# A streaming encoder layer on one core: the last norm with tokens on partitions and two store queues, the last 64 SWA keys on four quarters of the array

## The chip, the cores and the metric

The kernel runs on one core of a Trainium2 chip. TensorE (PE) does the matrix products, VectorE (DVE), ScalarE (ACT) and GpSimd (POOL) work element by element, SyncE (SP) issues most of the transfers, and 16 DMA engines move the data. The metric is the device time of one execution in microseconds (us), lower is better.

## The reference

One inference step of one encoder layer, for a prompt of 1024 frames and a sample of 64 frames, together 1088 tokens of width 1024, everything in float32:

```python
xn = rms_norm(x, g_attn); rq, rk, rv, rg, sq, sk, sv, ga, gb = split(xn @ w_in)
a = (rms_norm(retention(rq, rk, rv)) * silu(rg)) @ w_ret_out       # 4 heads of 256
b = swa_attend(sq, sk, sv) @ w_swa_out                             # sliding-window attention (SWA)
x += (sigmoid(ga) * a + sigmoid(gb) * b) @ w_mix_out
x += cross_attn(rms_norm(x, g_cross), memory)                      # 4 heads, 256 memory tokens
x += (silu(hn @ w_gate) * (hn @ w_up)) @ w_down                    # hn = rms_norm(x, g_ffn)
y = rms_norm(x, g_final)
```

Two places of it matter here. In the SWA a chunk of 64 queries sees 192 keys (its own chunk and the two before), with 16 query heads of 64 in 2 groups, each group with one key and one value head; the outcome for a group is p @ v with p of 512 rows (8 heads x 64 queries) by 192 keys and v of 192 keys by 64. There are 17 chunks, 16 of the prompt and one of the sample; the first two of the prompt see fewer keys. The last norm is y * rsqrt(mean(y * y) + 1e-6) * g_final over the 1024 features of a token.

## The kernel before

Activations lie with features on partitions: eight tiles of 128 features by 1088 tokens. Most products are split into a high part (rounded to the matmul type fp32r) and a low part, and made as three products (`mm3`, L156 to L158): high by high, high by low, low by high. A weight unit of 128 output features is loaded as `raw`, cast on ACT to the high part (L123) and subtracted on DVE for the low part (L124); SWA's own products are plain f32 ones.

The stages follow one another: projections (to some 811 us), SWA with filler (to some 1020), the merge of both branches, cross attention, and a feed-forward part with Strassen products, which ends in the norm (`finish`).

**SWA** (`swa`) runs over half chunks, 34 of them, in a hand-written pipeline; `in_order` and `issue_after` chain each piece behind the last matmul issued, so that PE's order is the one written out. For each half chunk there are `scores` (L969, and the softmax: L979/L982 on DVE, exponentials L990 on ACT, the division L996 on POOL), two steps later `turn` (transposes of the probabilities on PE, L1008 for the first 128 keys and L1018 for the last 64; copies L1012 on ACT and L1020 on DVE into `pT`), and, for every second half, `weigh` (L1031): p @ v for all 16 heads. `weigh` has two stages. Stage 1 has the first 128 keys, all 128 rows of the array and, for each value head v, 64 of its columns: two products of 512 columns. Stage 2 has the last 64 keys: value head 0 with the rows and columns 0 to 63, value head 1 with the rows and columns 64 to 127, again two products of 512 columns. They add into one PSUM bank, `pout`, which L1035 copies out on DVE:

```python
po = pw.tile([P, 512], F32, tag="out", name="pout")
for j, part in enumerate(parts):
    for v, (val, pT) in enumerate(part):
        self.last_mm = mm(po[rows[v], :], val[:, rows[v]], pT, start=j == 0, stop=j == len(parts) - 1).ins
```

In each step stand pieces of **filler** work (`filler`), which fills PE while the softmax goes on: the product with `w_ret_out`, in groups of one weight unit m by one chunk of tokens c (384, 384 and 320 columns). A group takes one PSUM bank `pd` from a pool of three (`plain_psum`), is run in two halves, and is evacuated on DVE (L1187), where it is multiplied by a gate and then stored to `d_mix`. Units 0 and 1 come with the first groups, units from m = 2 on are loaded when their first group's turn comes in the program; the buffers of `raw` are two, so that a unit's load waits for the casts of the unit two before. PSUM has eight banks; the SWA's own pool has five (`pss` 2, two for the transposes, `pout`) and `pd` three. The pool `pd` stays through the merge and the cross attention.

**The tail** (`finish`). The 1088 tokens are three ranges of columns: c = 0 and c = 1 (272 each) and c = 2 (544, whose product is done before). `grow` adds the last product to y (L1639) and squares it on ACT (L1643), `gather` sums the squares (L1648), and the norm is then made in one of two ways. For c = 2 and c = 0, `sums` (L1656) gives the sum over features by matmuls with the squares as weights and ones as data, so that tokens lie on partitions (128 x 3 or 128 x 5 numbers); `roots` makes 1/sqrt of these in five steps with one Newton step (`steps`, L1721 to L1726, the square root on ACT, L1722); `spread` (L1682, L1685) spreads the factors back along the partitions. For c = 1, the last to come, `wide_roots` (L1670, L1671) multiplies a matrix of ones by the squares, so that every partition has all sums, and makes the same five steps on 128 x 272 numbers. Each `scale` (L1689, DVE) multiplies a tile by its gain and the factors, and stores it through SP's queue (L120). `queued` chains DVE's work in the order written.

## Time and profile before

| | us |
|---|---|
| median of 3 runs (lowest, highest) | 2211.39 (2210.66, 2214.1) |
| profiled execution, its own time | 2210.58 |
| its span in the profile | 2208.8 |
| mean granted TensorE clock | 0.992 |

Line numbers L... are those of the kernel before. In the rows of a timeline stand the start and the length in us, the engine, the line, the operation, the tiles (written <- read), the shape and the number of records; in brackets what the engine was idle for and what released it. In the rows of groups stand the busy time, the mean of one in ns, and the idle time before them. PEld is TensorE's weight load, SPq SyncE's queue of transfers. Names like `pout` are those of the program's tiles.

### The profile page before, as it was taken

What the parts mean: (1) busy time and instruction counts of PE and PEld (TensorE: products, weight loads), DVE (VectorE), ACT (ScalarE), POOL (GpSimd) and SP (SyncE); (2) the same over time, 40 slices, a digit from 0 to 9 for tenths busy, and PEclk for the clock granted to TensorE, in tenths of its full rate; (3) what the DMA queues carried; (4) which work ended last, traced back from release to release, by engine and by line L of the source; (5) the groups of instructions that cost most, each with busy time, mean ns of one, the idle gap of its engine ahead of it and who ended that gap; (6) DMA issues with size and microseconds to landing.
All of it is one profiled execution on the core that took longest, in us unless ns stands there. A gap on an engine that the chain in (4) does not pass through costs nothing.

```text
span 2208.8 us, 41446 instructions
## 1 busy us (share of the span) xinstructions
PE 2155.7 (98%) x16307; PEld 2089.8 (95%) x16307; DVE 1577.8 (71%) x2654; ACT 875.8 (40%) x1894; POOL 653.2 (30%) x442
## 2 busy tenths in 40 slices
PE   8999999999999998999999999999999999999996
PEld 8999999999999996779999999999999999999996
DVE  7996958776677668775455555768777776778498
ACT  7344424344344346553133333333322222344243
POOL 1322333332343122230000000014555555544440
PEclk9999999999999999999999999999999999999998
DMA  5534253445245476327443111422333332385233
GB/s 197 167 127 137 90 149 122 131 127 156 96 153 172 165 220 213 112 64 224 124 153 107 57 49 58 144 86 90 124 133 101 104 118 95 124 297 167 91 114 110
DMA packets 181444, 290.83 MB, mean 132 GB/s; under 512 B 40290, under 2 KB 109314, under 8 KB 181250
## 3 DMA queue, kind: packets, MB, share of 16 engines
q1 hardware_dynamic: 176706, 278.74, 39.5%
q10 hardware_dynamic: 4032, 7.80, 0.9%
q8 instruction: 129, 2.11, 0.4%
q0 software_dynamic: 512, 1.64, 0.2%
q14 instruction: 65, 0.53, 0.1%
HBM read 196.95 MB, written 91.16 MB: 130 GB/s over the span
## 4 chain that ended last, share of the span: by engine, by line
PE 80%; DVE 11%; DMA 4%; ACT 2%; issue 2%; POOL 1%; SPq 0%; DVEq 0%; ACTq 0%; POOLq 0%
PE pq L215 15%; PE pq L212 15%; PE pq L213 15%; PE pd L156 8%; PE pd L158 8%; PE pd L157 8%; DVE wq L124 1%; PE pout L1031 1%; PE pss L969 1%; DMA hl<-d_op 1%; DVE T L124 1%; DVE B L124 1%; PE pp L1008 1%; DMA qs<-d_qkv 1%; DVE stage L596 1%
## 5 line engine op out<-in xcount | busy, mean ns | idle before, releaser
L124 DVE TENSOR_TENSOR wq<-raw,wq 128x512 fp32r<-128x512 f32 (+1 forms) x499 | 441.2, 888 | 137.1 <-ACT wq L123 135.5
L123 ACT CAST wq<-raw 128x512 fp32r<-128x512 f32 (+1 forms) x499 | 303.6, 614 | 586.0 <-PE pq L215 244.8
L212 PE MATMUL pq<-T,wq 128*128 128x272 f32 x1832 | 490.8, 288 | 3.6 <-ACT wq L123 2.1
L213 PE MATMUL pq<-T,wq 128*128 128x272 f32 x1832 | 491.5, 288 | 0.0
L213 PE MATMUL pq<-B,wq 128*128 128x272 f32 x1592 | 429.6, 290 | 6.7 <-DVE B L124 6.7
L212 PE MATMUL pq<-B,wq 128*128 128x272 f32 x1592 | 427.4, 289 | 1.3 <-DVE stage L596 1.1
L215 PE MATMUL pq<-T,wq 128*128 128x272 f32 x1832 | 382.0, 289 | 0.9 <-DVE wq L124 0.9
L190 POOL TENSOR_TENSOR raw<-raw 128x512 f32<-128x512 f32 (+1 forms) x59 | 90.2, 1529 | 967.1 <-DVE rs_r L301 480.4
L212 PEld LDWEIGHTS pq<-T,wq 128*128 128x128 f32 x1832 | 344.1, 188 | 5.6 <-ACT wq L123 1.9
L213 PEld LDWEIGHTS pq<-T,wq 128*128 128x128 f32 x1832 | 344.1, 188 | 0.8 <-issue 0.7
L215 PE MATMUL pq<-B,wq 128*128 128x272 f32 x1592 | 332.8, 289 | 0.0
L213 PEld LDWEIGHTS pq<-B,wq 128*128 128x128 f32 x1592 | 300.7, 189 | 9.2 <-DVE B L124 8.3
L212 PEld LDWEIGHTS pq<-B,wq 128*128 128x128 f32 x1592 | 300.5, 189 | 1.8 <-ACT wq L123 1.3
L215 PEld LDWEIGHTS pq<-T,wq 128*128 128x128 f32 x1832 | 289.6, 189 | 1.6 <-DVE wq L124 1.1
L215 PEld LDWEIGHTS pq<-B,wq 128*128 128x128 f32 x1592 | 252.8, 190 | 0.8 <-issue 0.8
L259 DVE TENSOR_TENSOR u<-pq,u 128x544 f32<-128x544 f32 x177 | 127.5, 720 | 101.3 <-PE pq L215 100.4
L193 POOL TENSOR_TENSOR raw<-raw 128x512 f32<-128x512 f32 (+1 forms) x59 | 82.8, 1403 | 110.4 <-DVE wq L124 105.3
L596 DVE TENSOR_TENSOR stage<-pq,u 128x544 f32<-128x544 f32 x112 | 80.4, 718 | 34.6 <-PE pq L215 31.2
L191 POOL TENSOR_TENSOR raw<-raw 128x512 f32<-128x512 f32 (+1 forms) x59 | 90.4, 1533 | 3.5
L996 POOL TENSOR_TENSOR t<-t,den 128x768 f32<-128x768 f32 (+2 forms) x34 | 49.9, 1468 | 127.0 <-DVE den L994 51.9
L196 POOL TENSOR_TENSOR raw<-raw 128x512 f32<-128x512 f32 (+1 forms) x59 | 82.4, 1397 | 4.4
L990 ACT ACTIVATE t<-t,nm 128x192 f32<-128x192 f32 (+2 forms) x136 | 58.9, 434 | 45.5 <-DVE nm L985 45.5
(388 smaller groups left out, 4600.4 us busy)
## 6 DMA issues: line engine op xcount, KB each, us to landing
hl<-d_op SPq DMA_DIRECT2D x85, 272.0 KB, 4.7
d_qkv<-stage SPq DMA_DIRECT2D x44, 272.0 KB, 2.2
d_op<-stage SPq DMA_DIRECT2D x44, 272.0 KB, 2.1
d_op<-ht SPq DMA_DIRECT2D x44, 272.0 KB, 3.3
raw<-w_gate SPq DMA_DIRECT2D x22, 512.0 KB, 3.5
raw<-w_up SPq DMA_DIRECT2D x22, 512.0 KB, 3.7
raw<-w_down SPq DMA_DIRECT2D x16, 512.0 KB, 4.1
d_gate<-stage ACTq DMA_DIRECT2D x28, 272.0 KB, 2.9
```

What stands on the lines that cost most here:

```text
L123: self.last_cast = self.nc.scalar.copy(hi, src).ins
L124: return self.nc.vector.tensor_tensor(out=lo, in0=src, in1=hi.bitcast(F32), op=ALU.subtract).ins
L156: mm(ps, wh, xh, start=start, stop=False)
L157: mm(ps, wh, xl, start=False, stop=False)
L158: self.last_mm = mm(ps, wl, xh, start=False, stop=stop).ins
L190: tt(out=a11, in0=a11, in1=a21, op=sub)
L191: tt(out=a21, in0=a21, in1=a22, op=add)
L212: mm(ps[:, c, :HC], w[:, 0, ks], x[:, 0, cs], start=start, stop=False)
L213: mm(ps[:, c, :HC], w[:, 0, ks], x[:, 1, cs], start=False, stop=False)
L215: self.last_mm = mm(ps[:, c, :HC], w[:, 1, ks], x[:, 0, c * HC:(c + 1) * HC], start=False, stop=stop).ins
L259: add = lambda out, a, b: nc.vector.tensor_tensor(out=out, in0=a, in1=b, op=ALU.add)
L596: nc.vector.tensor_tensor(out=o, in0=ps, in1=sb, op=ALU.add)
```

## The change

There are three parts.

*SWA.* `pout` becomes two banks, of which 256 columns each are used; each 512-column product is split into two of 256 columns (h = 0, 1: the first and the second half of `pT`), bank h taking half h. Stage 1 then has four products. In stage 2 the transposes of the second half of a chunk (hf = 1) put the two value heads on the opposite rows, so that the four products of stage 2 stand on four different quarters of the array: for h = 0 (rows 0 to 63, head 0) and (rows 64 to 127, head 1), for h = 1 (rows 64 to 127, head 0) and (rows 0 to 63, head 1). For the bank, the pool `pd` has two in place of three during SWA; the merge and the cross attention have three as before.

*Filler.* The third weight unit (m = 2) is made under `issue_after(first)`, where `first` is the evacuation L1187 of the first group. On DVE its low parts then stand behind that evacuation. The load of the unit two later, which needs the same buffer, comes later on SP, behind a load of queries and one store of `d_mix`.

*Tail.* `wide_roots` is gone; c = 1 goes by `sums`, `roots` and `spread` as the others do. `sums` takes the last tile's squares as a second product in the same accumulation. The scales of c = 0, and those of c = 1 on DVE, read the factors from PSUM where `spread` put them (c = 0 has no copy on ACT). One scale of c = 0 stands between the square root and the reciprocal of c = 1. The last tile of c = 2 gets its gain on ACT (`gain`) and its factors on POOL (`aside`), and so do three of the eight tiles of c = 1 (third, fifth and eighth in order). The eight stores of c = 1 go alternately through SP's and ACT's queues.

```diff
@@ -395,8 +395,10 @@
                 self.sixth, self.turns, self.held, self.last_held = None, 0, [], 0
                 self.wp = self.left.enter_context(tc.tile_pool(name="weights", bufs=2, reuse_waits="tile"))
                 self.project_phase()
+                with self.plain_psum(2, side="right"):
+                    self.swa_phase()
                 with self.plain_psum(side="right"):
-                    self.mix_phase()
+                    self.merge_swa()
                     self.mem.close()
                     self.cross_phase()
                 rp = sctx.enter_context(tc.tile_pool(name="rf", bufs=1, reuse_waits="tile", side="right"))
@@ -410,9 +412,9 @@
         self.fp = ctx.enter_context(self.tc.tile_pool(name="fa", bufs=1, reuse_waits="tile"))
 
     @contextmanager
-    def plain_psum(self, **where):
+    def plain_psum(self, bufs=3, **where):
         with ExitStack() as ctx:
-            pd = ctx.enter_context(self.tc.tile_pool(name="pd", bufs=3, reuse_waits="tile", space=PSUM, **where))
+            pd = ctx.enter_context(self.tc.tile_pool(name="pd", bufs=bufs, reuse_waits="tile", space=PSUM, **where))
             self.dense_psum = lambda: pd.tile([P, 512], F32, tag="d", name="pd")
             yield
 
...
@@ -1010,29 +1011,32 @@
                     live[c, "T"] = [self.pw2.tile([P, 2, 512], F32, tag="pT0", name="pT"), self.pw2.tile([P, 512], F32, tag="pT1", name="pT")]
                 pT = live[c, "T"][0][:n]
                 nc.scalar.copy(pT[:, :, hf * 256:(hf + 1) * 256], pp[:n, :].rearrange("p (v i) -> p v i", v=2))
-                parts = [[(vt[0][:n], pT[:, v, :]) for v in range(2)]]
+                cs = [slice(h * 256, (h + 1) * 256) for h in range(2)]
+                parts = [[(h, v, vt[0][:n], pT[:, v, cs[h]]) for h in range(2) for v in range(2)]]
                 if nk == NKEY:
                     pp = pw.tile([P, 512], F32, tag="pt1", name="pp")
-                    for v, i in reversed(units):
-                        k0, n = (64, P) if v else (P, 64)
-                        self.last_mm = nc.tensor.transpose(pp[:n, i * P:(i + 1) * P], t[:, v, i, k0:k0 + n], self.ident).ins
+                    for r in (1, 0):
+                        k0, n = (64, P) if r else (P, 64)
+                        for i in range(2):
+                            self.last_mm = nc.tensor.transpose(pp[:n, i * P:(i + 1) * P], t[:, r ^ hf, i, k0:k0 + n], self.ident).ins
                     pT = live[c, "T"][1]
                     nc.vector.tensor_copy(pT[:, hf * 256:(hf + 1) * 256], pp[:, :256])
-                    parts.append([(vt[2 - v][rows[v]], pT[rows[v]]) for v in range(2)])
+                    parts.append([(h, r ^ h, vt[2 - r][rows[r]], pT[rows[r], cs[h]]) for h in range(2) for r in (h, 1 - h)])
                 live[c, "parts"] = parts
 
             def weigh(c, hf):
                 if hf == 0:
                     return
                 parts = live.pop((c, "parts"))
-                po = pw.tile([P, 512], F32, tag="out", name="pout")
+                po = pw.tile([P, 2, 512], F32, tag="out", name="pout")
                 for j, part in enumerate(parts):
-                    for v, (val, pT) in enumerate(part):
-                        self.last_mm = mm(po[rows[v], :], val[:, rows[v]], pT, start=j == 0, stop=j == len(parts) - 1).ins
+                    for h, v, val, pT in part:
+                        self.last_mm = mm(po[rows[v], h, :256], val[:, rows[v]], pT, start=j == 0, stop=j == len(parts) - 1).ins
                 if c % 2 == 0:
                     outs["osb"] = sw.tile([P, KT, 2, 64], F32, tag="osb", bufs=2, name="osb")
                 osb = outs["osb"]
-                nc.vector.tensor_copy(osb[:, :, c % 2, :], po.rearrange("p (m q) -> p m q", q=64))
+                nc.vector.tensor_copy(osb[:, :, c % 2, :].rearrange("p (h m) q -> p h m q", h=2),
+                                      po[:, :, :256].rearrange("p h (m q) -> p h m q", q=64))
                 if c % 2 == 1 or c == 16:
                     n = 128 if c % 2 == 1 else 64
                     c0 = (c // 2) * P
@@ -1174,7 +1178,11 @@
             for m, c in order:
                 c0, n = CH[c]
                 if m not in units:
-                    units[m] = self.unit(io["w_ret_out"][m], KT)
+                    if m == 2:
+                        with tc.issue_after(first):
+                            units[m] = self.unit(io["w_ret_out"][m], KT)
+                    else:
+                        units[m] = self.unit(io["w_ret_out"][m], KT)
                 u, g = units[m], ld()
                 self.load(g[:, :n], self.d_gate[1][m, :, c0:c0 + n])
                 for ps in self.pieces(u, rets, c0, n):
@@ -1184,7 +1192,9 @@
                     step += 1
                     if ps is None:
                         yield
-                nc.vector.tensor_tensor(out=g[:, :n], in0=ps, in1=g[:, :n], op=ALU.mult)
+                ins = nc.vector.tensor_tensor(out=g[:, :n], in0=ps, in1=g[:, :n], op=ALU.mult).ins
+                if step == 2:
+                    first = ins
                 self.store(self.d_mix[m, :, c0:c0 + n], g[:, :n])
                 yield
 
@@ -1647,32 +1657,25 @@
             acc = self.rstd[:, cols[c]]
             self.queued(lambda: tt(out=acc, in0=acc, in1=squares[c, m], op=ALU.add))
 
-        def sums(c):
+        def sums(c, *more):
 
             spans = self.spans(cols[c].stop - cols[c].start)
             ps = bank()[:, :2 * len(spans)].rearrange("p (t two) -> p t two", two=2)
+            parts = [self.rstd[:, cols[c]], *more]
             for i, (a, w) in enumerate(spans):
-                a += cols[c].start
-                self.last_mm = nc.tensor.matmul(ps[:, i, :], self.rstd[:, a:a + w], self.ones[:, :2], start=True, stop=True).ins
+                for j, x in enumerate(parts):
+                    self.last_mm = nc.tensor.matmul(ps[:, i, :], x[:, a:a + w], self.ones[:, :2], start=j == 0,
+                                                    stop=j == len(parts) - 1).ins
             r = self.np.tile([P, 5], F32, tag="rf", bufs=2, name="rs_f")[:, :len(spans)]
             factors[c] = r, spans, ps[:, :, 0]
 
-        def roots(c):
+        def roots(c, between=None):
             r, spans, ps = factors[c]
             v = self.np.tile([P, 5], F32, tag="vf", bufs=2, name="rf_v")[:, :len(spans)]
             t = self.np.tile([P, 5], F32, tag="tf", bufs=2, name="rf_t")[:, :len(spans)]
-            self.steps(r, v, t, ps)
-
-        def wide_roots(c, m):
-
-            ps = bank()[:, :HC]
-            mm = nc.tensor.matmul
-            mm(ps, self.ones, self.rstd[:, cols[c]], start=True, stop=False)
-            self.last_mm = mm(ps, self.ones, squares[c, m], start=False, stop=True).ins
-            v, t = (self.hl.tile([P, HALF], F32, tag="hl", name="wide")[:, :HC] for _ in range(2))
-            self.steps(self.rstd[:, cols[c]], v, t, ps)
-
-        def spread(c):
+            self.steps(r, v, t, ps, between)
+
+        def spread(c, copied=True):
             r, spans, _ = factors[c]
             for part in ((0, 2), (2, 5)) if len(spans) > 4 else ((0, len(spans)),):
                 pb = bank()
@@ -1682,12 +1685,24 @@
                     self.last_mm = nc.tensor.matmul(pb[:, at:at + P], r[:, i:i + 1].broadcast_to([P, P]), self.ident,
                                                     start=True, stop=True).ins
                 c0 = cols[c].start
-                nc.scalar.copy(self.rstd[:, c0 + a0:c0 + a1], pb[:, :a1 - a0])
-
-        def scale(c, k):
+                if copied:
+                    nc.scalar.copy(self.rstd[:, c0 + a0:c0 + a1], pb[:, :a1 - a0])
+            return pb
+
+        def scale(c, k, by=None, queue=nc.sync):
             o = y[k][:, cols[c]]
-            self.queued(lambda: stt(o, o, self.gains[:, 3, k:k + 1], self.rstd[:, cols[c]], ALU.mult, ALU.mult))
-            self.store(self.io["o_y"][k, :, cols[c]], o)
+            by = self.rstd[:, cols[c]] if by is None else by
+            self.queued(lambda: stt(o, o, self.gains[:, 3, k:k + 1], by, ALU.mult, ALU.mult))
+            queue.dma_start(self.io["o_y"][k, :, cols[c]], o)
+
+        def gain(c, k):
+            o = y[k][:, cols[c]]
+            nc.scalar.mul(o, o, self.gains[:, 3, k:k + 1])
+
+        def aside(c, k, queue=nc.sync):
+            o = y[k][:, cols[c]]
+            nc.gpsimd.tensor_tensor(out=o, in0=o, in1=self.rstd[:, cols[c]], op=ALU.mult)
+            queue.dma_start(self.io["o_y"][k, :, cols[c]], o)
 
         for j in range(2 * KT):
             c, m = divmod(j, KT)
@@ -1704,22 +1719,40 @@
                 self.in_order(lambda: sums(0))
                 roots(0)
             if j == KT + 6:
-                self.in_order(lambda: spread(0))
-            if j >= KT:
-                scale(2, j - KT)
-        for k in range(3):
-            scale(0, k)
-        self.in_order(lambda: wide_roots(1, rest[-1][0]))
+                pb0 = self.in_order(lambda: spread(0, False))[:, :HC]
+            if c and m < KT - 1:
+                scale(2, m)
+            if c and KT - 5 < m < KT - 1:
+                gain(1, rest[m][0])
+            if j == 2 * KT - 2:
+                gain(2, KT - 1)
+                aside(2, KT - 1)
+        m = rest[-1][0]
+        spare = [rest[i][0] for i in range(KT - 4, KT - 1)]
+        scale(0, 0, pb0)
+        scale(0, 1, pb0)
+        self.in_order(lambda: sums(1, squares[1, m]))
+        roots(1, lambda: scale(0, 2, pb0))
         for k in range(3, KT):
-            scale(0, k)
-        for k in range(KT):
-            scale(1, k)
-
-    def steps(self, out, v, t, ps):
+            scale(0, k, pb0)
+        pb = self.in_order(lambda: spread(1))[:, :HC]
+        queues = [nc.sync, nc.scalar]
+        rows = [k for k in range(KT) if k not in spare]
+        for i, k in zip((2, 4, 7), spare):
+            rows.insert(i, k)
+        for i, k in enumerate(rows):
+            if k in spare:
+                aside(1, k, queues[i % 2])
+            else:
+                scale(1, k, pb, queues[i % 2])
+
+    def steps(self, out, v, t, ps, between=None):
         nc = self.nc
         stt, q = nc.vector.scalar_tensor_tensor, self.queued
         q(lambda: nc.vector.tensor_scalar(v, ps, 1.0 / D, EPS, ALU.mult, ALU.add))
         nc.scalar.activation(out, v, AF.Sqrt)
+        if between is not None:
+            between()
         q(lambda: nc.vector.reciprocal(out, out))
         q(lambda: nc.vector.tensor_tensor(out=t, in0=out, in1=out, op=ALU.mult))
         q(lambda: stt(t, t, -0.5, v, ALU.mult, ALU.mult))
```

More of the change, by code (lines that the diff above doesn't have):

```diff
@@ L886, in stage_tiles, with swa_phase @@
                 for t in self.ring_tiles(0, 2, "stage", F32) for i in range(2) for j in range(2)]
-    def mix_phase(self):
+    def swa_phase(self):
         with ExitStack() as ctx:
@@ L905, in mix_phase @@
             self.swa(ctx, fill())
-        self.merge_swa()
     def in_order(self, emit):
```

## Prediction

> **What bounds the kernel now.** I read the page's busy shares first, then the busy time by windows over the sliding-window (SWA) stage, then what TensorE waited for there, then two timelines: one chunk's value products, and the last 15 us.
>
> ```profile
> span 2208.8 us, 41446 instructions
> PE 2155.7 (98%) x16307; PEld 2089.8 (95%) x16307; DVE 1577.8 (71%) x2654; ACT 875.8 (40%) x1894; POOL 653.2 (30%) x442
> 818.00:860.00 42.00, 35.47 (x222) 28.23 (x220) 33.58 (x79) 25.50 (x100) 10.95 (x11) 0.96 0.76 246
> ...
> 900.00:940.00 40.00, 40.00 (x268) 30.78 (x267) 31.05 (x65) 22.20 (x87) 11.31 (x8) 1.00 0.38 113
> 940.00:980.00 40.00, 40.00 (x265) 29.76 (x264) 28.12 (x65) 22.11 (x86) 12.02 (x8) 1.00 0.23 71
> ...
> PE pss L969 <- DVE t L982: 5.4, 2, 4.0
> PE pp L1008 <- POOL t L996: 1.3, 1, 1.3
> PE pss L969 <- DVE t L979: 0.9, 1, 0.9
> PE pout L1031 <- ACT pT L1012: 0.8, 2, 0.6
> PE pd L157 <- DVE ret L1115: 0.6, 1, 0.6
> ```
>
> In the SWA stage (a row has the window, its length, then the busy time of PE, PEld, DVE, ACT and POOL, and the granted clock) PE is never idle from 900 on, at full clock, with DVE busy for 28 to 31 of 40 us. What PE does less of there shortens the time one for one. The gaps lie at the stage's start: 6.5 us in the first window, and all waits of the stage add to 9.0. The tail has no PE work: there DVE and SP set the end.
>
> **The change, part by part.** The value products of one chunk (15 of 17 chunks have both stages):
>
> ```profile
> 940.47 0.65 PE L1031 MATMUL pout<-pT,swin 128*64 128x512 f32 x2
> 940.95 0.60 PE L1031 MATMUL pout<-pT,swin 128*64 128x512 f32 x2
> 941.48 0.65 PE L1031 MATMUL pout<-pT,swin 64*64 64x512 f32 x2
> 942.49 0.43 PE L969 MATMUL pss<-swin,swin 64*128 64x192 f32 x2
> 942.76 0.49 PE L969 MATMUL pss<-swin,swin 64*128 64x192 f32 x4
> 943.08 0.33 PE L969 MATMUL pss<-swin,swin 64*128 64x192 f32 x2
> ```
>
> An f32 product is two records, a first and a second pass. A row with x2 that is as long as one record (0.65, 0.43, 0.33) is two records that started together: two products on different parts of the array run at once. The four records of a stage thus take two slots: 940.47 to 940.95 and on to 941.48, where stage 2 starts, which hands over to the scores (pss) at 942.49. Each stage takes 1.01 us. The scores give the price of a column: two pairs start between 942.76 and 943.08, 0.16 each for 192 columns, 0.83 ns a column. A 512-column slot is then 0.427, two are 0.85, and 0.16 of a stage's 1.01 is its first weight load (0.05: the first slot is 0.48) and the change to another tile shape at its end (0.10: the second is 0.53).
>
> Stage 1 has four products of 256 columns in place of two of 512: twice the slots at half the length, and their weights are loaded under the slot before, as the scores' are, whose slots are shorter still. I cost it at nothing; if each of the two added slots showed a load of 0.05, it would be +0.1 a chunk, +1.7 in all. Stage 2 has four 256-column products on four different quarters. If all four run together it takes two slots of 0.213 and 0.16, 0.58 us: 0.427 less, times 15, **−6.4 us**. If only two run at once it stays at 1.01: 0. The scores are the nearest row: there two row halves of the array, each over all columns, write the same PSUM partitions in two banks at once, and four quarters at once would ask no more of PSUM than that. I take −6.4. L1018's transposes are as many, in another order; L1035's copy reads as many elements.
>
> The rule that speaks against this is in the Trainium skill, "TensorE: Matmul & The Clock Gate", Part 3: matmuls start and end strictly in program order. By it the four products' passes (first, second of each) would need five slots, 1.23 us, and the sum would have +3.3 in place of −6.4. By it the stage before would take three slots of 0.427 and 0.16, 1.44; it took 1.01, so the trace disagrees.
>
> pout now takes two PSUM banks and the filler's pd two instead of three. A filler group may then start only when the evacuation (L1187) of the group two before has ended, where it had three groups' time.
>
> ```profile
> L1187 DVE TENSOR_TENSOR swin<-pd,swin 128x384 f32<-128x384 f32 x16 | 8.9, 556 | 7.8 <-PE pd L158 7.6
> 914.89 0.34 PE L156 MATMUL pd<-ret,wq 128*128 128x384 f32 x1
> 915.09 0.56 DVE L1187 TENSOR_TENSOR swin<-pd,swin 128x384 f32<-128x384 f32 x1
> ```
>
> I replayed before's starts and evacuation ends with two banks. At 914.89 a group starts while the evacuation it would have to wait for ends at 915.65: 0.76 us late. One other is 0.4 late, some 0.3 more may come in the last chunk where DVE's order changes, those in the first groups fall into gaps that are there anyway, and the rest have 1.0 to 1.8 us to spare. Sum **+1.5**; ends 0.5 and, if each of the 23 L1187 groups (16 of 384 columns and 7 of 320) were 0.4 late, +9. While PE waits there, the scores and transposes behind it wait too.
>
> The third weight unit now comes after the first group's evacuation on DVE, and its second load on SP comes later, behind a query load and one store of d_mix.
>
> ```profile
> 829.71 1.14 ACT L123 CAST wq<-raw 128x512 fp32r<-128x512 f32 x2 [7.25 <-DMA raw<-w_ret_out]
> 830.36 1.29 DVE L124 TENSOR_TENSOR wq<-raw,wq 128x512 fp32r<-128x512 f32 x2 [3.75 <-ACT wq L123]
> 831.57 0.55 DVE L1187 TENSOR_TENSOR swin<-pd,swin 128x384 f32<-128x384 f32 x1
> 832.93 0.71 PE L969 MATMUL pss<-swin,swin 64*128 64x128 f32 x8 [3.96 <-DVE t L982]
> ```
>
> PE's longest gap, 3.96, ends on DVE work (t, L982) queued behind L1187 and the low parts (L124), which wait for casts that wait for the DMA. With L1187 (0.55) out of that queue L982 starts 0.5 earlier; what L982 waits for stays. The casts keep their order on ACT and the unit's later load is used a group later, so I see no new wait. **−0.7**, between −1.7 (if the 4 us of low parts behind go out of the way too) and +1 (late second load).
>
> Now the tail (DVE, then SP, then earlier rows of the same lines):
>
> ```profile
> 2193.41 0.78 DVE L1689 SCALAR_TENSOR_TENSOR y<-y,gains,rstd 128x544 f32<-128x544 f32 x1
> 2194.11 0.50 DVE L1689 SCALAR_TENSOR_TENSOR rstd_f<-rstd_f,gains,rstd 128x272 f32<-128x272 f32 x1
> 2195.34 0.44 DVE L1721 TENSOR_SCALAR wide<-pq 128x272 f32<-128x272 f32 x1
> 2196.28 1.85 DVE L1723 RECIPROCAL rstd<-rstd 128x272 f32<-128x272 f32 x1 [0.50 <-ACT rstd L1722]
> 2199.12 0.44 DVE L1726 SCALAR_TENSOR_TENSOR rstd<-wide,rstd 128x272 f32<-128x272 f32 x1
> 2199.48 2.15 DVE L1689 SCALAR_TENSOR_TENSOR y<-y,gains,rstd 128x272 f32<-128x272 f32 x5
> 2201.95 2.97 DVE L1689 SCALAR_TENSOR_TENSOR y<-y,gains,rstd 128x272 f32<-128x272 f32 x7
> ...
> 2202.88 3.38 SPq L120 DMA_DIRECT2D o_y<-y  x7
> ...
> 2186.71 0.16 DVE L1721 TENSOR_SCALAR rf_v<-pq 128x3 f32<-128x3 f32 x1
> 2187.75 0.16 DVE L1726 SCALAR_TENSOR_TENSOR rs_f<-rf_t,rs_f 128x3 f32<-128x3 f32 x1
> 2185.33 0.73 PE L1656 MATMUL pq<-ones,rstd 128*128 128x2 f32 x6
> 2189.42 0.83 PE L1682 MATMUL pq<-ident,rs_f 128*128 128x128 f32 x6
> 2154.43 1.02 POOL L191 TENSOR_TENSOR raw<-raw 128x384 f32<-128x384 f32 x1
> 2157.05 2.17 DVE L1554 TENSOR_TENSOR y<-u,y 128x544 f32<-128x544 f32 x2
> ```
>
> Before: roots on 128x272 from 2195.34 to 2199.56 (4.2 us, the reciprocal 1.85 of it), thirteen scales at 0.41, and SP's stores at 0.49 each (3.38 for 7), issued until 2206.26, behind DVE's end at 2204.92; the span ends 2.5 later. After: the 544-wide scale at 2193.41 (0.70) leaves DVE for ACT and POOL, early. There POOL runs beside DVE for some 1.5 us, and DVE operations with two SBUF inputs stretch beside POOL: L1554 took 2.17 for two at 2157.05, while POOL was on its last addition, against 0.78 for one of that width at 2193.41. I take a loss of 1.25 there, which with the 0.70 saved puts the last gather's end at 2194.0 instead of 2193.45. Then come six small sums, 12 records (0.73 for 6, so 1.4 to 1.5), under two scales: 2195.5. The roots on 128x3 take 1.20 (2186.71 to 2187.91), with one scale in the shadow of the square root, to 2196.9. The spread on PE (0.83) ends at 2197.85, under five scales of the first columns. From 2196.9 DVE has ten scales, 4.1 us: 2201.0. POOL's three rows (272 wide; 1.02 for 384 gives 0.75 to 0.95) end by 2200.8, and DVE beside them reads PSUM. SP has nine of the last 13 stores: issued until 2201.8, ACT's four until 2201.3. With 2.5 behind it the end is 2204.3: −4.5.
>
> ```profile
> DMA  0000000598988787878787878787887870000000
> q1 hardware_dynamic: 1872, 1.81, 53.0%
> o_y<-y SPq DMA_DIRECT2D x12, 136.0 KB, 1.8
> ```
>
> These stores already keep the DMA engines at 0.78 (a row of slices of 0.25 us, in tenths). At 0.495 a store, full use is 0.38 each; thirteen in 4.5 us is 0.34, so the last lands about 0.3 later. **−4.2**, between −3.2 (a slow POOL, the clash 1 us dearer) and −5.0 (no clash).
>
> The skill's rule that speaks against two store queues is in "DMA: Bandwidth & Descriptors", Issuing engines are not separate DMA queues: SP and ACT feed the same 16 DMA engines, so a second issuer saves issue time alone. By it the 0.3 above stands; without it the tail would be −4.5.
>
> Sum: −6.4 + 1.5 − 0.7 − 4.2 = **−9.8**. The profiled execution took 2210.58; 2200.8. The median, 2211.39, is 0.81 above it: **2201.6**. No change that a measurement could tell is 0.2%, 4.4 us: 2207.0 to 2215.8.
>
> **Rivals.** (1) Only pairs run: stage 2 stays, −3.4, 2208.0. For it: no row of before shows more than two records starting together. Three at once (three slots, −3.2 instead of −6.4): 2204.8. (2) Two banks starve the filler in steady state: +9 in place of +1.5, −2.3, 2209.1. DVE is free for 9 to 12 of 40 us there, which speaks against it; it decides once L1187 comes 1.0 to 1.8 us later than now. (3) Slower: products over the same PSUM partitions exclude one another, and the quarters go one by one. Eight slots of 0.213 and 0.16 is 1.87 for 1.01: +12.8 over 15 chunks, sum +9.4, 2220.8. It decides from 0.5 us per chunk. Against it stand the scores' pairs. (4) Strict program order: the five slots above in place of two, 1.23: sum −0.1, 2211.3.
>
> **How the numbers follow.** Forecast 0.66; three slots 0.05; pairs 0.10; starved filler 0.07 (0.03 of it faster, at half the price); one by one 0.09; strict order 0.03. Faster 0.66 + 0.05 + 0.03 = 0.74, same 0.10 + 0.04 + 0.03 = 0.17, slower 0.09. The forecast's own bounds: best −6.4 + 0.5 − 1.7 − 5.0 = −12.6, 2198.8; worst −6.4 + 1.7 (loads in stage 1) + 3 + 1 − 3.2 = −3.9, 2207.5. The range reaches to the pairs above: 2197.5 to 2208.5, which holds 0.84.
>
> **What would show it.** Records x4 starting within some 20 ns in stage 2, and 0.58 us from its start to the next work on PE; PE waits on L1187 of 1 to 2 us in all, and a first gap under 3.5 us; no 1.85 us reciprocal, and the end some 2.5 us after SP's last issue at about 2201.8 less what SWA gave. It is wrong if stage 2 keeps 1.01 or more, if PE idles on pd after 900, or if the last stores queue behind POOL.

## The result, and the profile after

The changed kernel takes 2206.7 us in the median of 13 runs (2199.33 to 2214.3), the kernel before 2213.08 in 13 runs beside it (2210.66 to 2217.11). The ratio, taken over all these runs, is 0.9967, with a 95% interval of 0.9955 to 0.9979: 7.3 us less, 4.6 to 10. The two medians by themselves are 6.4 us apart; where a gain is given below it is the ratio's. Two more series gave 0.9969 [0.9956, 0.9981] and 0.9965 [0.9953, 0.9978]. The profiled execution took 2199.33 us with a span of 2197.5; it is the fastest of its series, 7.4 below the median, while the profiled one of before was only 0.8 below the median of its own three runs. So a time of one stage can be read from these two profiles, but not the whole gain. In the changed kernel lines are numbered anew: L1034 is the value product (L1031), L970 the scores, L1009 and L1021 the transposes, L1195 the filler's evacuation (L1187), L1649 the last growth of y (L1639), L1667 the sums, L1685 and L1689 the spread and its copy, L1695 the scales, L1704 the multiplication on POOL.

The page of the changed kernel, its busy windows over SWA, and what PE waited for from 805 to 1015 us:

```profile
span 2197.5 us, 41725 instructions
PE 2151.3 (98%) x16449; PEld 2098.0 (95%) x16449; DVE 1574.3 (72%) x2650; ACT 876.6 (40%) x1898; POOL 646.0 (29%) x446
```

```profile
818.00:860.00 42.00, 35.84 (x251) 29.32 (x249) 35.64 (x79) 25.91 (x95) 12.17 (x12) 1.00 0.80 247
900.00:940.00 40.00, 40.00 (x306) 32.70 (x304) 30.85 (x69) 22.29 (x87) 12.27 (x8) 1.00 0.34 102
1020.00:1060.00 40.00, 38.99 (x239) 38.99 (x240) 23.94 (x46) 12.28 (x24) 0.00 (x0) 1.00 0.61 185
```

```profile
PE pss L970 <- DVE t L983: 3.9, 2, 2.4
PE pp L1009 <- POOL t L997: 2.3, 2, 1.8
PE pss L970 <- DVE t L980: 1.9, 1, 1.9
PE pout L1034 <- ACT pT L1013: 0.8, 1, 0.8
PE pd L156 <- DVE swin L1195: 0.3, 1, 0.3
```

The waits of SWA add to 9.2 us where they added to 9.0: the longest fell from 3.96 to 2.4, but POOL (0.5 of it new, at 989) and the next scores are waited for longer. The filler's two PSUM banks cost one wait of 0.3 us. The granted clock of the first window is 1.00 where it was 0.96. And PE, which never idled after 900 in the kernel before, loses 1 us behind 1020.

One chunk's value products in the timeline of the changed kernel (a row holds the records that run at one moment):

```profile
934.49 0.44 PE L1034 MATMUL pout<-pT,swin 128*64 128x256 f32 x2
934.76 0.60 PE L1034 MATMUL pout<-pT,swin 128*64 128x256 f32 x4
935.51 0.45 PE L1034 MATMUL pout<-pT,swin 64*64 64x256 f32 x4
935.77 0.40 PE L1034 MATMUL pout<-pT,swin 64*64 64x256 f32 x4
936.10 0.43 PE L970 MATMUL pss<-swin,swin 64*128 64x192 f32 x2
```

Stage 1 takes from 934.49 to 935.51, 1.02 us as before. In stage 2 four records start together (x4 in 0.45, where one takes 0.43), twice, and the scores start at 936.10: 0.59 us where it was 1.01.

The tail, with DVE first, then PE, ACT, POOL and the two queues:

```profile
2185.27 0.43 DVE L1649 TENSOR_TENSOR y<-pq,y 128x272 f32<-128x272 f32 x1
2186.38 0.49 DVE L1695 SCALAR_TENSOR_TENSOR y<-y,gains,pq 128x272 f32<-128x272 f32 x1
2187.74 0.16 DVE L1752 TENSOR_SCALAR rf_v<-pq 128x3 f32<-128x3 f32 x1 [0.87 <-PE pq L1667]
2188.90 2.12 DVE L1695 SCALAR_TENSOR_TENSOR y<-y,gains,pq 128x272 f32<-128x272 f32 x5
2191.56 1.72 DVE L1695 SCALAR_TENSOR_TENSOR y<-y,gains,pq 128x272 f32<-128x272 f32 x4
...
2186.11 0.38 PE L1667 MATMUL pq<-ones,rstd 128*128 128x2 f32 x2 [2.40 <-DVE rstd L1658]
2189.04 1.65 PE L1685 MATMUL pq<-ident,rs_f 128*128 128x128 f32 x6 [1.33 <-DVE rs_f L1759]
2190.73 0.39 ACT L1689 COPY rstd<-pq 128x272 f32<-128x272 f32 x1 [2.58 <-PE pq L1685]
2173.86 1.37 POOL L1704 TENSOR_TENSOR y<-y,rstd 128x544 f32<-128x544 f32 x1 [22.88 <-ACT rstd L1689]
2191.19 2.19 POOL L1704 TENSOR_TENSOR y<-y,rstd 128x272 f32<-128x272 f32 x3 [15.96 <-ACT rstd L1689]
2193.30 0.41 SPq L1696 DMA_DIRECT2D o_y<-y  x1
2193.57 0.58 ACTq L1705 DMA_DIRECT2D o_y<-y  x1
```

From the last growth of y to the end of the span it is 12.2 us (2185.27 to 2197.5), where it was 16.1 (2192.71 to 2208.8). The 128x272 roots are gone. But the spread takes 1.65 us, not 0.83, and the end comes 3.35 us after the last issue (2194.15), not 2.5.

### The profile page after: what moved, and what is told of

It is laid out like the page before. It is cut to its first block, busy times and chain, and to the rows that moved or that the text cites. A ratio compares the mean times of both kernels' runs of the same rounds, so it can differ in the third digit from the quotient of the medians.

```text
span 2197.5 us, 41725 instructions
## 1 busy us (share of the span) xinstructions
PE 2151.3 (98%) x16449; PEld 2098.0 (95%) x16449; DVE 1574.3 (72%) x2650; ACT 876.6 (40%) x1898; POOL 646.0 (29%) x446
## 4 chain that ended last, share of the span: by engine, by line
PE 75%; DVE 12%; DMA 5%; ACT 3%; issue 3%; POOL 1%; SPq 0%; POOLq 0%; DVEq 0%; ACTq 0%
PE pq L215 15%; PE pq L213 15%; PE pq L212 15%; PE pd L156 7%; PE pd L158 7%; PE pd L157 7%; DVE wq L124 2%; DMA hl<-d_op 1%; PE pss L970 1%; PE pout L1034 1%; DMA qs<-d_qkv 1%; DVE B L124 1%; DVE stage L598 1%; DVE u L259 1%; DVE stage L630 1%
## 5 line engine op out<-in xcount | busy, mean ns | idle before, releaser
L124 DVE TENSOR_TENSOR wq<-raw,wq 128x512 fp32r<-128x512 f32 (+1 forms) x499 | 446.0, 897 | 145.7 <-ACT wq L123 143.6
L190 POOL TENSOR_TENSOR raw<-raw 128x512 f32<-128x512 f32 (+1 forms) x59 | 78.1, 1323 | 971.8 <-DVE rs_r L301 481.8
L193 POOL TENSOR_TENSOR raw<-raw 128x512 f32<-128x512 f32 (+1 forms) x59 | 83.6, 1417 | 123.1 <-DVE wq L124 118.0
L191 POOL TENSOR_TENSOR raw<-raw 128x512 f32<-128x512 f32 (+1 forms) x59 | 90.2, 1529 | 3.5
L196 POOL TENSOR_TENSOR raw<-raw 128x512 f32<-128x512 f32 (+1 forms) x59 | 82.6, 1401 | 4.4
```

Of the source, the lines that this page charges most:

```text
L124: return self.nc.vector.tensor_tensor(out=lo, in0=src, in1=hi.bitcast(F32), op=ALU.subtract).ins
L191: tt(out=a21, in0=a21, in1=a22, op=add)
L193: tt(out=a11, in0=a22, in1=a11, op=sub)
```

## The experiments

Each ratio below is against the kernel before in the same series; kernels of different series are compared by their ratios. Since one execution differs from another by several us, each trace is cut into stages too. The stages are: SWA from its first scores to the fifth chunk's value products ("start", with the four quarters of two chunks in it), on to the last chunk's ("steady", 12 chunks), the wait at the merge's start, and the tail from the last growth of y on. They are read from each trace's first records of these lines; a merge wait of 0 means none of 0.4 us or more.

| kernel | ratio to before, 95% | start | steady | merge wait | tail |
|---|---|---|---|---|---|
| before | 1 | 67.9 | 122.9 | 0 | 16.1 |
| changed, first | 0.9967 [0.9955, 0.9979] | 65.3 | 118.6 | 1.4 | 12.2 |
| changed, second | 0.9969 [0.9956, 0.9981] | 67.4 | 118.6 | 1.2 | 12.1 |
| changed, third | 0.9965 [0.9953, 0.9978] | 67.0 | 118.6 | 2.1 | 13.4 |
| SWA alone | 0.9983 [0.9973, 0.9993] | 67.8 | 118.6 | 1.6 | 16.0 |
| tail alone | 0.9988 [0.9979, 0.9997] | 68.2 | 122.9 | 0 | 12.2 |
| pairs | 0.9978 [0.9967, 0.9989] | 65.3 | 123.1 | 1.8 | 12.2 |
| banks alone | 1.0014 [1.0003, 1.0024] | 67.5 | 123.0 | 0.4 | 16.1 |
| no unit | 0.9984 [0.9974, 0.9995] | 69.2 | 118.6 | 1.3 | 12.2 |
| one queue | 0.9979 [0.9969, 0.9989] | 67.8 | 118.6 | 1.8 | 13.4 |
| best | 0.9959 [0.9947, 0.9970] | 65.1 | 118.6 | 0 | 12.1 |
| warm only | 0.9967 [0.9952, 0.9982] | 67.5 | 118.5 | 2.0 | 13.4 |
| best, warm | 0.9970 [0.9957, 0.9983] | 69.8 | 118.6 | 0 | 12.5 |
| best, first nine | 0.9948 [0.9929, 0.9968] | 70.2 | 118.6 | 0 | 11.3 |

**The changed kernel again.** No edit.

> The changed kernel once more, for a second trace beside the first. The first profiled execution was 11.3 us shorter than before's, while the median of the runs was 6.4 us shorter, so some 5 us differ from execution to execution. Theory A (the stages outside the change vary): SWA and tail are as in the first profile (stage 2 of the value products 0.59 us, tail from the last growth of y to the end 12.2 us), and what is longer lies in waits on DMA in the projections and the feed-forward part, in before as in after. Theory B (PE arrives at the merge ahead of its loads): the wait before the first merge product, 1.4 us in the first profile and none before, is 4 to 8 us here. Median: 0.33% under before by both.

Its span was 2206.6, 9.1 more than in the first profile. Of this 0.3 lie ahead of SWA, 2.1 in the start of SWA, 0.9 in the merge's product with `w_swa_out`, 1.2 in the rest of the merge and the cross attention, 4.7 in the feed-forward part, and none in the tail or in the steady part of SWA. Theory B falls: the merge's wait was 1.2 us here. Theory A holds in the main, but the start of SWA, which the change touches, varies too.

**One part each.** SWA alone is the first three hunks and those of `swa`; tail alone those of `finish`. Pairs is the changed kernel with stage 2 on the diagonal:

```diff
-                    parts.append([(h, r ^ h, vt[2 - r][rows[r]], pT[rows[r], cs[h]]) for h in range(2) for r in (h, 1 - h)])
+                    parts.append([(h, v, vt[2 - v][rows[v]], pT[rows[v], cs[h]]) for h in range(2) for v in range(2)])
```

with the transposes as before.

> Before, with only the SWA part (pout of two banks, four quarters, pd of two banks); the filler's third unit and the tail are as before. Theory A (the parts add): 15 times 0.42 = -6.3 us in SWA, less the merge start's +2.0: -4.3 us, some 2208.8 against 2213.1; the stage's first gap stays near 4 us, and the clock falls there as before. Theory B (the gain is lost at the merge start): within 2 us of before. Tail 16.1 us from the last growth of y to the end.

> Before, with only the tail's part. Theory A: -3.9 us (16.1 to 12.2 from the last growth of y to the end), with the spread of the factors at half clock (1.65 us) and the DMA engines over 0.9 busy; SWA as before. Theory B says the same of the tail. If the tail's gain came from the earlier work of POOL and ACT in other parts of after, it would be under 2 us here.

> The changed kernel with the last 64 keys on the diagonal quarters only, as before: four products of 256 columns in two pairs, two banks as in the change. Theory A (the gain in SWA comes from four quarters at once): stage 2 takes 1.01 us again, +0.42 x 15 = +6.3 us against the changed kernel in SWA, less what the merge start then waits less (2.0): +4.3 to +6.3. If the gain came from the banks or the halves: no difference from the changed kernel.

A chunk's value products in the timeline of pairs:

```profile
939.76 2.10 PE L1033 MATMUL pout<-pT,swin 128*64 128x256 f32 x16
```

The parts add within the noise: 0.17% and 0.12%, each with some 0.1 either way, against 0.31 to 0.35% together. In pairs the sixteen records span 2.10 us, so both stages take 1.01 again, and the steady part is 123.1 instead of 118.6. Twelve stages of 0.42 are 5.0; the missing 0.5 is the new wait on POOL, which pairs doesn't have. The halves and the banks alone gain nothing; four quarters at once do. What the ratios say of pairs (2.0 us over the changed kernel in the same series, with intervals of 2.4 or more on either side of each) is less than the 4.3 expected; it does not contradict it, and by itself would not show it. The tail's gain is the tail's own.

The wait at the merge is only in part what I took it for. In pairs the steady part is as slow as in before, and PE waits 1.8 us there all the same. The timeline of the changed kernel shows what ends the wait:

```profile
1019.84 1.89 ACT L123 CAST swa<-ld 128x320 fp32r<-128x320 f32 x4 [1.89 <-DMA ld<-d_swa]
1021.01 0.62 PE L156 MATMUL pd<-swa,wq 128*128 128x384 f32 x2 [1.43 <-ACT swa L123]
```

The operand of the merge has eight tiles, of which the last two of the first chunk are cast late, behind a cast that waits for its load. In PE's order the first product that waits for these two tiles is number 52 of the merge in before and in tail alone, but number 45 in every kernel that has pd and pout in their new sizes, banks alone among them (best and its successors, below, have it as number 55). The scheduler put seven products, 1.2 us of cover, behind the stall.

The order is not the whole of it. In banks alone, with the same order, the wait is 0.4:

```profile
1030.04 0.45 PE L156 MATMUL pd<-swa,wq 128*128 128x384 f32 x1 [0.40 <-ACT swa L123]
```

The other part is when the first of the two casts starts: 7.8 to 8.3 us after the merge's first product in before, tail alone and banks alone, but 8.6 to 9.9 us after it in the kernels that wait longer, pairs (9.05) and the changed kernel (8.58 to 9.54) among them. All of these come to the merge earlier, 201 to 206 us after SWA's first scores instead of 208 to 209. So PE may well come ahead of its loads in part, by up to some 1.6 us (9.9 less 8.3); why the loads don't keep up was not tried.

**Banks, the filler's unit, one queue.** Banks alone is before with

```diff
-                po = pw.tile([P, 512], F32, tag="out", name="pout")
+                po = pw.tile([P, 2, 512], F32, tag="out", name="pout")[:, 0, :]
```

and pd of two banks in SWA. No unit is the changed kernel without `issue_after(first)`. One queue has `queues = [nc.sync, nc.sync]`.

> Before, with only the banks moved: pout takes two PSUM banks, of which one is used, the filler's pd has two during SWA; products, filler and tail as in before. Theory A (two pd banks suffice): waits of PE on the filler's evacuation stay under 1 us in all, SWA within 1 us of before. Theory B (my replay): +1.2 to +1.5 us. In both the merge's first products are ordered by the same scheduler: if the merge's wait comes with the pools' change and not with the quarters, PE waits 1 to 2 us for the casts of the SWA operands here too, though SWA ends no earlier than in before.

> The changed kernel without its filler part: the third unit's low parts stand ahead of the first evacuation on DVE again. Theory A (this part gains by itself): the first long gap in SWA is 3.5 to 4 us again instead of 2.2 to 2.4, and the granted clock falls behind it as in before, so SWA up to the middle of its second chunk is 1.5 to 2 us later than in the changed kernel; the whole run +1.5 to +2. Theory B (the gap's shortening is given back in the waits that follow at POOL and DVE): under 0.5 us.

> The changed kernel with all eight last stores on SP's queue. Theory A (the second queue takes issue time off the end): SP issues until some 12.2 - 3.35 + 2.3 us after the last growth of y, as 13 stores at 0.49 us from the end of the roots on take 6.4 us where two queues took 4.9 to 5.2; the end is +1.0 to +1.5 us (tail 13.2 to 13.7 against 12.2). Theory B (the DMA engines, over 0.9 busy in the changed kernel, set the end whatever queue issues): tail within 0.4 of 12.2.

Banks alone shows no cost in SWA (start and steady 190.4 against 190.8). At the merge I had expected a wait of 1 to 2 us and it is 0.4. By the ratio it is 0.14% slower, 3 us, and the trace has no place for them; that stays open.

With two banks and the old order of the unit, PE's longest gap is a wait for the first group's evacuation, as in no unit:

```profile
PE pd L156 <- DVE swin L1191: 4.6, 1, 4.6
```

In the two kernels that have the quarters, two banks and the old order (SWA alone, no unit) that gap is 3.83 and 4.62 us, and the start 67.8 and 69.2. In the eight that have the quarters and the new order it is 1.78 to 3.55, and the start 65.1 to 70.2, in the mean 67.5. So the gap is some 1.8 us shorter, and the start some 1.0, less than the start varies by itself: the next waits grow (POOL 2.3 instead of 1.3 and the scores 1.9 instead of 0.9 in the changed kernel, against before), and the rest hangs in good part on the clock. In windows of 30 us from 10 us after the first scores, of before, of the changed kernel and of best, first nine:

```profile
821.50:851.50 30.00, 24.04 (x147) 19.52 (x147) 23.97 (x54) 16.47 (x60) 7.82 (x9) 0.94 0.81 264
```

```profile
820.60:850.60 30.00, 24.72 (x170) 20.14 (x168) 26.14 (x57) 16.24 (x59) 7.52 (x8) 1.00 0.85 268
```

```profile
822.30:852.30 30.00, 24.87 (x154) 20.73 (x153) 24.37 (x55) 17.23 (x61) 6.98 (x8) 0.89 0.82 260
```

In these windows the clock (third number from the end) fell in all five kernels of the old order. Of the eight with the new one it fell in five, for gaps from 1.79 us on, and did not in three, with gaps of 1.78 to 2.40. Over the whole of the start the clock was 1.00 in the first profile of the changed kernel and in best, whose starts are the shortest of the kernels with the quarters (65.3 and 65.1), and 0.90 in best, warm and in best, first nine, whose starts are the longest (69.8 and 70.2). So neither theory stands as written: part of the shorter gap is given back, and a fall of the clock is made less sure, not ruled out. By the ratios no unit is some 3.7 us slower than the changed kernel, more than its stages explain; with intervals of 2 to 3 us on either side, and the two in different series, it stays open how much of that is the part.

With one queue SP issues all eight last stores, the last at 2206.95:

```profile
2206.95 0.40 SPq L1705 DMA_DIRECT2D o_y<-y  x1
```

Its tail of 13.4 holds 0.2 us of slower sums. From the end of the roots (2200.68) to the end of the span (2210.2) it is 9.5 us, where the changed kernel has 8.5 (2188.98 to 2197.5). The second queue is worth 1.0 us, as theory A said, at its lower end: from the end of the roots the last issue ends 1.5 us sooner (5.2 us after it instead of 6.7), and lands 0.5 later behind that (3.35 instead of 2.85).

**A version with the merge and the tail mended.** Best runs the first three groups of the merge over their first six tiles, then over the last two (54 products ahead of the late casts), and has four scales of the first columns ahead of the last sums:

```diff
-            for m, u, (c0, n) in self.m_major(unit("w_swa_out"), CH, lead=2):
+            work = self.m_major(unit("w_swa_out"), CH, lead=2)
+            head = [next(work) + (self.dense_psum(),) for i in range(3)]
+            for ks in (range(KT - 2), range(KT - 2, KT)):
+                for m, u, (c0, n), ps in head:
+                    for k in ks:
...
-        scale(0, 0, pb0)
-        scale(0, 1, pb0)
+        for k in range(4):
+            scale(0, k, pb0)
```

> The changed kernel with two additions. In the merge the first three groups run their first six tiles each, and then the last two tiles, which are cast last: 54 products before the first that needs the late casts, where the scheduler had put 45. Theory A: the wait of 1.2 to 1.8 us there becomes 0 to 0.3. In the tail four scales of the first columns stand before the last sums in place of two, so that DVE does not idle 0.87 us and two stores start in time in which the DMA engines are idle: tail 11.4 to 11.8 us from the last growth of y, against 12.2. Together -1.5 to -2.2 against the changed kernel. Theory B (the late casts depend on when SP issues their loads, and the tail on the last scales alone): no gain in either place.

The merge's wait is gone, here and in the two later versions built on this one. The tail is 12.1, no better: the time that DVE no longer idled ahead of the sums came back ahead of the last scales, behind the slow spread and its copy, in the timeline of best:

```profile
2191.15 1.65 PE L1692 MATMUL pq<-ident,rs_f 128*128 128x128 f32 x6 [1.33 <-DVE rs_f L1766]
2193.26 0.50 DVE L1702 SCALAR_TENSOR_TENSOR rstd_f<-rstd_f,gains,pq 128x272 f32<-128x272 f32 x1 [0.94 <-ACT rstd L1696]
```

**The clock in the tail.** In the changed kernel the granted clock falls to 0.5 towards the end of the sums, and the spread takes twice its time, in the busy windows:

```profile
2187.70:2191.00 3.30, 1.66 (x7) 1.36 (x6) 3.16 (x11) 0.48 (x2) 0.00 (x0) 0.50 0.49 158
```

In the third profile of it the clock fell before the sums, and these were slow too (a pair of records 0.59 in place of 0.38; the sums end 2.6 us after their start, not 1.6), for a tail of 13.4:

```profile
2196.73 0.59 PE L1667 MATMUL pq<-ones,rstd 128*128 128x2 f32 x2 [2.41 <-DVE rstd L1658]
2200.78 1.65 PE L1685 MATMUL pq<-ident,rs_f 128*128 128x128 f32 x6 [1.33 <-DVE rs_f L1759]
```

The next kernels fill PE's gaps there with products of ones by ones that nothing reads, nine ahead of the sums and five behind (warm only; best, warm), then nine alone (best, first nine):

```diff
+            pair = self.bank_pair()
+            warm = lambda: nc.tensor.matmul(pair[:, 1, :P], self.ones, self.ones, start=True, stop=True).ins
+            for i in range(idle[0]):
+                self.last_mm = self.in_order(warm)
```

> The changed kernel with 14 products of ones by ones in the tail, whose outcome nothing reads: nine between the last product and the last sums, five between the sums and the spread, to keep TensorE busy in its gaps of 2.40 and 1.33 us. Theory A (the spread takes 1.65 us instead of 0.87 because the granted clock is 0.5 after the gaps): the spread takes 0.83 to 0.9 us at clock 1.00, the factors are copied 0.8 us earlier, POOL's three rows end 0.8 earlier, and the tail is 11.5 to 11.9 us against 12.2, less than 0.8 shorter since DVE's scales and the DMA engines come next. Theory B (the spread is slow by its shape or by PSUM): it stays at 1.65 us and the tail at 12.2.

> The version with the late tiles last in the merge and four scales ahead of the last sums, and with the same 14 products in the tail. In that version DVE idled 0.94 us before the first scale of the last columns, behind the slow spread and its copy. Theory A: this wait falls to 0.2 or less, tail 11.2 to 11.5 us against 12.1. Theory B (the DMA engines set the end): tail over 11.9. Whole run -0.4 to -0.5% against before by A.

The spread became 0.93 us long at clock 1.00, so the cause is the clock. The tail did not become shorter, through a fault of the experiment: the five products behind the sums write a tile that DVE reads next, and DVE waited for them. In the timeline of warm only:

```profile
2200.54 0.16 DVE L1758 TENSOR_SCALAR rf_v<-pq 128x3 f32<-128x3 f32 x1 [2.00 <-PE pq L1665]
2201.84 0.93 PE L1691 MATMUL pq<-ident,rs_f 128*128 128x128 f32 x6 [1.33 <-DVE rs_f L1765]
```

> The version with the late tiles last and four scales ahead, with only the nine products of ones ahead of the last sums. In the two runs before, the five behind the sums wrote a tile that DVE reads next, and DVE waited 1.2 to 2.0 us for them; without them that wait is gone. Theory A (the clock falls for a gap of 2.40 us, not for the 1.33 that stays): the spread takes 0.9 us, DVE waits 0.2 or less before the last scales, tail 11.3 to 11.6 us from the last growth of y, against 12.2 in the changed kernel and 12.1 without the nine. Theory B (it is the gap of 1.33 next to the spread that counts): the spread takes 1.65 us, tail 12.1. Against before: -0.40 to -0.50%.

> The changed kernel a third time, on the same chip and beside the version above. Tail 12.1 to 12.3, merge with a wait of 1.2 to 1.8 us on the casts, stage 2 of the value products 0.59 us. The version above should be 2 to 2.7 us faster by the stages' sum (merge 1.5 to 2, tail 0.7), which the medians can hardly tell.

The timeline of best, first nine:

```profile
2187.47 2.17 PE L1672 MATMUL pq<-ones 128*128 128x128 f32 x18
2192.88 0.93 PE L1698 MATMUL pq<-ident,rs_f 128*128 128x128 f32 x6 [1.33 <-DVE rs_f L1772]
2194.27 0.50 DVE L1708 SCALAR_TENSOR_TENSOR rstd_f<-rstd_f,gains,pq 128x272 f32<-128x272 f32 x1 [0.22 <-ACT rstd L1702]
```

The gap of 1.33 us stays and the clock does not fall before the spread's end; the spread is fast, DVE waits 0.22 instead of 0.94, and the tail is 11.3. This is one profile; that the gap of 2.40 was always followed by a fall rests on eight. Its median is 2202.97 (6 runs) beside 2207.76 of the changed kernel and 2214.58 of before: 0.9948 [0.9929, 0.9968]. It has the shortest tail, no wait in the merge and the lowest ratio of all kernels here, though its start was the longest. Against the changed kernel the intervals overlap (0.9965 [0.9953, 0.9978]); by the stages it is shorter by 0.9 to 2.1 in the tail and 1.2 to 2.1 in the merge.

## Why the prediction was right, and where its terms were off

The forecast was 2201.6, a gain of 9.8 us; the median came to 2206.7, and the measured gain is 7.3 (4.6 to 10). The likeliest case happened: the four quarters run together. Term by term:

- **Four quarters, −6.4.** Measured 0.42 for 15 chunks, −6.3. The price of a column from the scores' pairs, and the fixed 0.16 of a stage, gave 0.58 for a stage that took 0.59. Stage 1 cost nothing, as said. Of the 6.3, 0.5 went into the new wait on POOL. The rivals of pairs, of three slots, of one by one and of strict order are out, and the starved filler with them: after 900 PE waits for an evacuation nowhere.
- **Two PSUM banks, +1.5, and the filler's unit, −0.7.** Together I had +0.8. In the mean of eight kernels the start is 67.5, where it was 67.9 and 68.2 in the two with before's SWA; 0.85 of that gain are the quarters of two chunks, so the two parts together cost some 0.3, with 2 us either way by the chance of the clock. (The +3 for the banks in the worst case has no working of its own.) The banks' term was mis-sized in its place: the late evacuations at which I had counted 0.76 and 0.40 were waited for nowhere in the steady part, and the cost lies in the first group's evacuation, which the unit's new place takes off. The unit's step "what L982 waits for stays" stopped too soon: the next waits grew.
- **The tail, −4.2.** Measured −3.9 in five of the six profiles that have this tail unaltered, −2.7 in the sixth (the changed kernel's third), −3.7 in the mean. The sum came out near by errors against each other, which is luck. The clash of POOL with DVE, charged with 0.55 on balance, came to no more than 0.23 on one addition at 2174.87 (0.66 instead of 0.43): POOL had done its 544-wide row by 2175.23, long before the end. From the last growth of y to the end of the roots it took 3.7 us, where I had 4.2. But the spread took 1.65, not 0.83, since I took its price from a place where the clock was full; here it fell behind PE's gap of 2.4 us. Of these 0.8 only 0.3 came through to the last issue (5.2 us behind the roots, where I had 4.9). And the last landing was 0.85 later than in before, where I had 0.3.
- **The merge, not in the sum.** This is the term that was missing, +1.2 to +2.1 us. The prediction has terms for SWA, the filler and the tail and none for the merge, and gives no reason for that; it does not ask what the pools' new sizes do to the order of products at the merge's start, nor whether the merge's loads keep up when SWA ends earlier. It is the largest single error.

By the stages' means: start −0.6, steady −4.4, the last chunk −0.4 (stage 2), merge +1.6, tail −3.7, together −7.5, where the ratio says −7.3. Without the merge it would have been −9.1, against the −9.8 of the forecast.

The two rules of the Trainium skill came out differently. "TensorE: Matmul & The Clock Gate", Part 3, has matmuls start strictly in program order; the x4 rows and the 0.59 us show that the first passes of four products on different quarters start within 21 ns of each other, and their second passes follow together 0.27 us later, though the kernel calls each product, both passes, before the next. "DMA: Bandwidth & Descriptors", on issuing engines that share the same DMA engines, agrees: against one queue the second saved 1.5 us of issue time, the landing came 0.5 later, and 1.0 us was left.

## What to carry to other kernels

Price a packed product from records that already run side by side in the same trace: slot time from the column count, plus the fixed loss at a change of tile shape; that held to 0.01 us here. When a pool's size changes, look through the whole order that the scheduler makes of it, also stages away: seven products that changed places took 1.2 us of cover from late casts, and with the casts' own delay the wait cost 1.6 us, a fifth of the gain. And take the price of a small matmul chain from a place with the same idle time ahead of it, because in this tail the clock halved behind a gap of 2.4 us.

## What the hardware showed unexpectedly

- Four f32 products of 256 columns on four 64x64 quarters start 7 ns apart and end 7 ns apart, while products from different rows of the array write the same 64 PSUM partitions in two banks, and others one bank in different partitions: 0.59 us for what took 1.01 in two pairs of 512.
- The granted clock fell to 0.5 behind gaps of PE of about 2 us, but not each time, and some time after the gap's start: in SWA it fell behind a gap of 1.79 us and not behind one of 2.40; in SWA's first 10 us it fell in eight of the fourteen profiles, where no gap was longer than 1.48 us and all fourteen have that one. So the length of one gap does not decide it. In the tail it fell in all eight profiles that have the gap of 2.4 us, once ahead of the sums and otherwise amid or behind them. With nine products of ones, which leave a gap of 0.40, it stayed at full speed through a gap of 1.33 in the one profile that has this.
